# A bank pair emptied into a small tile, masks selected on POOL, and convolution steps that pause: a hybrid attention and mLSTM layer on one NeuronCore

## The chip, the core and the metric

The program runs on one core of a Trainium2 chip. The core has engines with queues of their own: PE (matmul, with its weight loads shown as PEld), DVE and ACT (elementwise work), POOL, and SP, which here only issues DMAs. PE writes its products to PSUM, eight banks of 512 fp32 columns; DVE and ACT read them there, POOL works on SBUF alone. The metric is the device time of one execution in microseconds.

## The reference

One encoder layer on two sequences of 1024 and 2048 tokens, each with the same 16 meta tokens ahead. After a norm, one projection feeds two branches, neighbourhood attention and a bidirectional mLSTM; their gated outputs are merged, projected and normed.

```python
xn = _rmsnorm(h, g_pre)
proj = xn @ w_in + b_in
na_q, na_k, na_v, na_z, ml_qk, ml_v, ml_z, ml_o, ml_g, mg = jnp.split(proj, SPLIT_IDX, axis=-1)
ya = (_neighbourhood_attention(na_q, na_k, na_v, na_rpb) * silu(na_z)) @ w_a
yb = (_mlstm_branch(ml_qk, ml_v, ml_g, ml_o, ml_conv_w, ml_head_g) * silu(ml_z)) @ w_b
y = (ga * ya + gb * yb) @ w_out
return h + _rmsnorm(y, g_post)
```

The mLSTM branch first runs a convolution of three taps along the tokens over `ml_qk` and a SiLU. Then, in each direction, every chunk of tokens has a masked decay matrix and a state carried from the chunks before:

```python
logD = jnp.where(lower, b[..., :, None] - b[..., None, :] + ig[..., None, :], NEG)
S = jnp.einsum('bhnjd,bhnsd->bhnjs', q, k) * jnp.exp(logD - m_t[..., None])
num = einsum(S, v) + e_inter * einsum(Cs, q)
h = num / maximum(abs(den), exp(-m_t))
```

## The kernel before

**Precision.** Every fp32 operand is split into a rounded part and a rest (`h` and `l`: `xh` and `xl`, `whi` and `wlo`, `sh` and `sl`), ACT rounding and DVE subtracting, and PE forms two or three products of the parts (`mm3`, L180 to L182).

**Two streams.** `run` interleaves two generators. `dense` is the projection and the final products, by `PLAN`: a first group of columns of sequence 0, then the stage "S" (`sstream`), which computes the other columns of sequence 0 with seven products in place of eight, then the groups of sequence 1, then `final`. `sparse` is, by `STEPS`, the mLSTM of sequence 0, its attention, and the same two for sequence 1. PE's order is the order in which the code is written out; the order on the other engines is made by the planner, except that `behind` pins an instruction after the one traced before it on its engine. Each engine works through its queue in order.

**Steps between matmuls.** After every piece of a column job the code calls `beside` (L542), which advances work for the other engines. `pstep` (called at L545 and L547) advances one convolution by one step: `cprep` loads a stretch of `mq` or `mk`, waits some turns, scales by ACT (L1584), adds two taps by DVE (L1587), takes a tanh (L1589), multiplies (L1591) and stores to `qk`. Two convolutions are under way at a time. `cpreps` queues those of sequence 0 during the first group and those of sequence 1 when their columns are done.

**Splitting x.** `build_half` loads four parts of x for 512 tokens, scales them (L519), and after the word "scaled" splits each into `xh` (ACT, L526) and `xl` (DVE, L527). `sbegin` does the same for stage S.

**Stage S.** `sorder` sets the order of the units: 1, 6, 5, 2, 7 and so on for the first set of columns. `ssum` forms sums of weight quarters on DVE (L854), which ACT (L272) and DVE (L273) then split.

**mLSTM.** `ml_gates` makes the gate factors; for each of four heads `ml_states` makes the chunks' state sums and `ml_outputs` the outputs, in blocks `b` of two chunks of 128 tokens, five turns to a block. `load` fetches `um` (128 partitions, 2 chunks x 2 directions x 128); `mask` adds 0 or -1e30 to it (L1780), `decay` takes the exponential (ACT, L1786), `weigh` multiplies by the scores and splits (`sh`, `sl`). `back(b, j)` for each chunk writes the state's part to a `tr` bank and, by ACT with a factor (L1849), to `num`; then four products (L1852, L1853) fill `pa`, a pair of PSUM banks of which there is only one pair (the pool `pl`); DVE adds both halves of it to `num` (L1855, L1856). `finish` divides, `ml_norm` norms. The pair `pa` is also used in `ml_states`.

Of the kernel before, what the change touches and what calls it, by code (L numbers as in the profile page):

```python
# [10 lines left out]
F32 = mybir.dt.float32  # L11
F32R = mybir.dt.float32r
I32 = mybir.dt.int32
AF = mybir.ActivationFunctionType
ALU = mybir.AluOpType
# [3 lines left out]
P = 128  # L19
# [9 lines left out]
BIG = 1e30  # L29
# [8 lines left out]
CB = 2  # L38
# [88 lines left out]
class K:  # L127
# [3 lines left out]
    def __init__(self, tc, ins, outs):  # L131
        self.tc, self.nc = tc, tc.nc
        self.xs = []
        self.i, self.o = ins, outs
        self.wreq, self.wraw, self.wrdy, self.wout = deque(), deque(), deque(), 0
        self.wseen, self.wkept, self.xkept = set(), {}, {}
        self.rwait = {}
        self.xput, self.turn, self.last, self.turns = deque(), 0, None, False
        self.need, self.gpost = False, None
        self.pq, self.pact = deque(), deque()  # L140
        self.have, self.rtag = {}, "tr"
        self.fmend = {C_MK + 3 * P: "a", C_NK + 3 * P: "k", C_NQ + 3 * P: "q", C_NZ + 3 * P: "z"}
        self.bg, self.XF, self.XS, self.sb, self.staged = deque(), {}, {}, {}, deque()
        self.hold, self.early = deque(), True
        self.rpre, self.xhold = {}, True


    def rsqrt8(self, pool, v, shape):
# [304 lines left out]
    def build_half(self, s, t0, res):  # L453

        nc, wp = self.nc, self.wp
        if (s, t0) in self.xkept:
            yield
            yield "scaled"
            x = []
            for name, part in zip(("xh", "xl"), self.xkept[s, t0]):  # L460
                x.append(wp.tile([P, KT, HALF], F32R, name=name, bufs=2))
                for k in range(0, KT, 4):
                    nc.sync.dma_start(x[-1][:, k:k + 4, :512].bitcast(F32), part[:, k:k + 4, :])
                yield
            res.append(tuple(x))
            return
        if (s, t0) in self.XF:
            xts = [self.xfload(self.XF[s, t0], e) for e in range(4)]
            yield
            yield "scaled"  # L470
            x = self.xparts()
            for e in range(4):
                h = x[0][:, 2 * e:2 * e + 2, :512]
                self.behind(nc.scalar.activation(h, xts[e], AF.Copy))
                self.behind(nc.vector.tensor_tensor(x[1][:, 2 * e:2 * e + 2, :512], xts[e], h.bitcast(F32), op=ALU.subtract))
                yield
            res.append(tuple(x))
            self.xkeep(s, t0, x)
            return
        if s == 0:  # L480
            xts = self.xnext or [self.xtload(s, t0, e, wp, 4) for e in range(4)]
            self.xnext = None
            while self.rwait:
                yield "wait"
            self.early = False
            yield "scaled"
            g = self.gpre
            if not self.done:
                p = self.psum("sm", [P, 512])
                nc.tensor.matmul(p[:, :KT], self.ident, g, start=True, stop=True)  # L490
                g = self.cp.tile([P, KT], F32, name="gx")
                nc.vector.tensor_copy(g, p[:, :KT])
            x, r = self.xparts(), []
            for e in range(4):
                self.xsplit(x, xts[e], e, 0, g)
                if not self.done:
                    self.wflush(2)
                yield
            res.append(tuple(x))
            if self.done:  # L500
                return
            yield from self.rsum(self.toks, r)
            nc.vector.tensor_copy(self.rc[:, 4:8], r[0])
            dg = self.rdiag(r[0], self.toks[0][0])

            def rows():
                self.rrows(dg, self.rr[:, 1], "sm")
                self.xp.close()
            self.rwait[s, t0] = rows
        else:  # L510
            xts = [self.xtload(s, t0, e, wp, 4) for e in range(4)]
            yield
            yield
            rr = wp.tile([P, 512], F32, name="rx", tag="thT", bufs=1)
            self.rrows(self.rpre.pop((s, t0)), rr, self.rtag)
            yield
            for k in range(KT):
                v = xts[k // 2][:, k % 2]
                self.behind(nc.vector.scalar_tensor_tensor(v, v, self.gpre[:, k:k + 1], rr, op0=ALU.mult, op1=ALU.mult))  # L519
                if k % 2:  # L520
                    yield
            yield "scaled"
            x = self.xparts(t0 % 1024 == 0)
            for e in range(4):
                h = x[0][:, 2 * e:2 * e + 2, :512]
                self.behind(nc.scalar.activation(h, xts[e], AF.Copy))  # L526
                self.behind(nc.vector.tensor_tensor(x[1][:, 2 * e:2 * e + 2, :512], xts[e], h.bitcast(F32), op=ALU.subtract))  # L527
                yield
            res.append(tuple(x))
            self.xkeep(s, t0, x)  # L530

# [10 lines left out]
    def beside(self):  # L542

        self.turn += 1
        self.pstep()  # L545
        if (1, 0) in self.have:
            self.pstep()  # L547
        if self.bg and self.turn % 2 == 0:
            if next(self.bg[0], "end") == "end":
# [503 lines left out]
    def sstream(self, visits, nxt):  # L1053

        nc = self.nc
# [7 lines left out]
        for n, u in self.sorder(visits):  # L1063
            s, t0, c, v = self.sdq[n]
# [14 lines left out]
                            self.sstage(*visits[v + 1][:2], w)  # L1079
            q = self.sq[n]  # L1080
            if u == 7 and not n:
                self.sbload(1)
            tm = c in TMAJ
            form = ("p (k c) -> p k c", dict(k=4)) if tm else ("p (a k c) -> p a k c", dict(a=2, k=4))
# [95 lines left out]
    def group(self, s, t0, meta, cols, reuse, nxt):  # L1180
# [4 lines left out]
        for j, (kind, c) in enumerate(jobs):  # L1185
# [21 lines left out]
            for hf in range(2):  # L1207
# [2 lines left out]
                    side = self.spread(self.build_half(*todo[1][:2], self.xs), 15)  # L1210
                elif last and nxt and nxt[0] == "S":
                    if hf == 0:
                        while self.bg:
                            if next(self.bg[0], "end") == "end":
                                self.bg.popleft()
# [398 lines left out]
    def ml(self, s):  # L1614
# [3 lines left out]
        with tc.tile_pool(name=f"mg{s}", bufs=1, side="right", reuse_waits="tile") as keep:  # L1618
            with tc.tile_pool(name=f"mt{s}", bufs=1, side="right", reuse_waits="tile") as mp:
                self.tri = keep.tile([P, 2, P], F32, name="tri")  # L1620
                nc.sync.dma_start(self.tri, self.i["tri"])
                self.trim = keep.tile([P, CB, 2, P], F32, name="trim")
                for j in range(CB):
                    nc.sync.dma_start(self.trim[:, j], self.i["trimask"])
                g = []
                yield from self.ml_gates(s, keep, mp, g)
            self.small(False)
# [115 lines left out]
    def ml_outputs(self, mp, s, h, g, NB, sts, norms):  # L1743
# [33 lines left out]

        def mask(b):
            if b < NB:
                self.behind(nc.vector.tensor_tensor(ums[b], ums[b], self.trim, op=ALU.add))  # L1780

        def decay(b):
            if b < NB:
# [54 lines left out]
        def back(b, j):  # L1838
# [10 lines left out]
                nc.scalar.activation(num[:, j, d], pi[:, 130 * d:130 * d + 130], AF.Copy, scale=g[d]["e"][:, cc, h:h + 1])  # L1849
            pa = self.pl.tile([P, 2, 512], F32, name="pa")  # L1850
            for d in range(2):
                nc.tensor.matmul(pa[:, d, 0:258], sh[:, j, d, :], v[:, j].rearrange("p a c -> p (a c)")[:, 0:258], start=True, stop=True, skip_group_check=True)  # L1852
                nc.tensor.matmul(pa[:, d, 0:130], sl[:, j, d, :], v[:, j, 0], start=False, stop=True, skip_group_check=True)  # L1853
            nj = num[:, j]
            nc.vector.tensor_tensor(nj, pa[:, :, 0:130], nj, op=ALU.add)  # L1855
            nc.vector.tensor_tensor(nj[:, :, 0:P], pa[:, :, 130:258], nj[:, :, 0:P], op=ALU.add)  # L1856

        def finish(b):
            num = nums.pop(b)
# [429 lines left out]
```

## Time and profile before

| | |
|---|---|
| three runs: lowest, median, highest | 2721.04, 2722.5, 2722.78 us |
| the profiled execution, its own time | 2714.73 us |
| its span, from the first to the last instruction | 2713.0 us |
| instructions in the span | 47274 |

The profile is of one execution. Its page gives busy times of each engine and the groups of instructions; the trace behind it gives each instruction's start, its duration, and, in brackets, how long its engine was idle just before it and which instruction ended that. A matmul's duration overlaps the next one's, so distances between starts are read where single gaps are meant. A line of the form `L1852` is a line of the kernel before.

### The profile page before, as it was taken

To read this page: it belongs to the slowest core of one execution; us is meant where nothing else is said; L and a number is where in the kernel's file an instruction comes from. 1 tells how busy PE (TensorE), PEld (TensorE's weight loads), DVE (VectorE), ACT (ScalarE), POOL (GpSimd) and SP (SyncE) were. 2 spreads that over 40 slices of the span, in tenths; PEclk is the share of its full clock that TensorE was granted. 3 is DMA by queue.
4 is the path that set the end of the run, shared out by engine and by line. 5 is a ranking of instruction groups with operands and counts; after the bars stand their busy time and mean duration, and the time that the engine had idled before them with its cause. 6 is when DMAs were issued, how large, how long until landed. Compare 5 with 4: busy or idle time off the path is not lost.

```text
span 2713.0 us, 47274 instructions
## 1 busy us (share of the span) xinstructions
PE 2671.5 (98%) x16504; PEld 2376.4 (88%) x16504; DVE 1792.7 (66%) x4424; ACT 1517.0 (56%) x3375; POOL 124.8 (5%) x294
## 2 busy tenths in 40 slices
PE   9999999999999999999999999999999999999998
PEld 7999988879998789998878888888889898989888
DVE  5557765545777746775424868575668879787764
ACT  5233354435555556666534756565548676777641
POOL 0005000005000004000000000000000000000000
PEclk9999999999999999999999999999999999999999
DMA  9984454369865797766576666786589999898955
GB/s 375 338 280 140 141 191 153 101 236 344 268 216 175 249 333 219 216 209 198 183 261 200 212 232 205 234 295 205 177 291 339 316 304 296 250 324 245 314 210 220
DMA packets 351507, 657.51 MB, mean 242 GB/s; under 512 B 53445, under 2 KB 158869, under 8 KB 351269
## 3 DMA queue, kind: packets, MB, share of 16 engines
q1 hardware_dynamic: 344004, 645.46, 71.4%
q0 software_dynamic: 7264, 9.04, 1.2%
q8 instruction: 130, 2.13, 0.3%
q14 instruction: 109, 0.88, 0.1%
HBM read 438.64 MB, written 215.66 MB: 241 GB/s over the span
## 4 chain that ended last, share of the span: by engine, by line
PE 82%; DMA 8%; DVE 6%; ACT 3%; issue 1%; SPq 0%; POOL 0%; DVEq 0%; ACTq 0%; POOLq 0%
PE pj L180 13%; PE pj L181 13%; PE pj L182 13%; PE pj L658 5%; PE pj L660 5%; PE pj L659 5%; PE sm L1424 2%; PE pj L2066 2%; PE pj L2064 2%; PE pj L2065 2%; PE tr L1410 2%; DMA tg<-gt 1%; PE pa L1852 1%; DMA kr<-nkm 1%; PE sm L182 1%
## 5 line engine op out<-in xcount | busy, mean ns | idle before, releaser
L180 PE MATMUL pj<-xh,whi 128*128 128x512 f32 (+1 forms) x1480 | 581.2, 393 | 3.8 <-ACT st L581 2.4
L181 PE MATMUL pj<-xl,whi 128*128 128x512 f32 (+1 forms) x1480 | 566.6, 383 | 0.4 <-DVE xl L357 0.4
L182 PE MATMUL pj<-xh,wlo 128*128 128x512 f32 (+1 forms) x1480 | 565.7, 382 | 0.3 <-DVE wlo L284 0.3
L658 PE MATMUL pj<-whi,xh 128*128 128x256 f32 (+1 forms) x1152 | 330.8, 287 | 0.0
L182 PEld LDWEIGHTS pj<-xh,wlo 128*128 128x128 f32 x1480 | 278.8, 188 | 58.3 <-DVE wlo L284 0.5
L180 PEld LDWEIGHTS pj<-xh,whi 128*128 128x128 f32 x1480 | 278.8, 188 | 53.4 <-ACT st L581 3.1
L659 PE MATMUL pj<-wlo,xh 128*128 128x256 f32 (+1 forms) x1152 | 324.8, 282 | 0.0
L660 PE MATMUL pj<-whi,xl 128*128 128x256 f32 (+1 forms) x1152 | 324.8, 282 | 0.0
L181 PEld LDWEIGHTS pj<-xl,whi 128*128 128x128 f32 x1480 | 279.3, 189 | 46.5 <-issue 0.7
L2064 PE MATMUL pj<-whi,mh 128*128 128x256 f32 x768 | 219.8, 286 | 0.0
L658 PEld LDWEIGHTS pj<-whi,xh 128*128 128x128 f32 x1152 | 217.2, 189 | 0.4
L659 PEld LDWEIGHTS pj<-wlo,xh 128*128 128x128 f32 x1152 | 217.1, 188 | 0.2
L660 PEld LDWEIGHTS pj<-whi,xl 128*128 128x128 f32 x1152 | 217.0, 188 | 0.0
L2065 PE MATMUL pj<-wlo,mh 128*128 128x256 f32 x768 | 216.5, 282 | 0.0
L2066 PE MATMUL pj<-whi,mlo 128*128 128x256 f32 x768 | 216.5, 282 | 0.0
L1413 DVE TENSOR_TENSOR pts<-tr,pts 96x384 fp32r<-96x384 f32 (+2 forms) x192 | 118.5, 617 | 65.4 <-ACT pts L1412 64.6
L180 PE MATMUL pj<-yh,whi 128*128 128x512 f32 x384 | 154.1, 401 | 0.7 <-ACT yh L1436 0.7
L181 PE MATMUL pj<-yl,whi 128*128 128x512 f32 x384 | 151.0, 393 | 0.2 <-DVE yl L1437 0.2
L182 PE MATMUL pj<-yh,wlo 128*128 128x512 f32 x384 | 151.0, 393 | 0.0
L2065 PEld LDWEIGHTS pj<-wlo,mh 128*128 128x128 f32 x768 | 145.5, 189 | 1.0
L2064 PEld LDWEIGHTS pj<-whi,mh 128*128 128x128 f32 x768 | 145.4, 189 | 1.0
L2066 PEld LDWEIGHTS pj<-whi,mlo 128*128 128x128 f32 x768 | 145.4, 189 | 0.0
(459 smaller groups left out, 6106.8 us busy)
## 6 DMA issues: line engine op xcount, KB each, us to landing
whi<-wh SPq DMA_DIRECT2D x140, 512.0 KB
wlo<-wl SPq DMA_DIRECT2D x140, 512.0 KB
wraw<-wu SPq DMA_DIRECT2D x64, 512.0 KB
wh<-whi SPq DMA_DIRECT2D x64, 512.0 KB
wl<-wlo SPq DMA_DIRECT2D x64, 512.0 KB
gt<-st SPq DMA_DIRECT2D x96, 256.0 KB
tg<-gt SPq DMA_DIRECT2D x96, 256.0 KB
xt<-xt SPq DMA_DIRECT2D x32, 512.0 KB
```

Source lines behind the costliest of these rows:

```text
L180: mm(out, ah, bh, start=start, stop=False, **more)
L181: mm(out, ah, bl, start=False, stop=False, **more)
L182: mm(out, al, bh, start=False, stop=stop, **more)
L658: nc.tensor.matmul(o, xh, wh, start=k == 0 and not (pair and a), stop=False, skip_group_check=True)
L659: nc.tensor.matmul(o, xh, wl, start=False, stop=False, skip_group_check=True)
L660: nc.tensor.matmul(o, xl, wh, start=False, stop=k == KT - 1, skip_group_check=True)
L1410: nc.tensor.transpose(pt[:ks, ch, :], pr_[:, ch * ks:(ch + 1) * ks], self.ident)
L1413: nc.vector.tensor_tensor(pts[:ks, :nb, 1, :], pt[:ks, :nb], pts[:ks, :nb, 0, :].bitcast(F32), op=ALU.subtract)
L1424: nc.tensor.matmul(av[:, cb % 2], vt[:ks, kc // 8 + ch].rearrange("p a b -> p (a b)"), pts[:ks, ch].rearrange("p a b -> p (a b)"), start=c ...
L2064: nc.tensor.matmul(o, mh[:, f, xs], q, start=fresh and f == 0, stop=False, skip_group_check=True)
L2065: nc.tensor.matmul(o, mh[:, f, xs], w[1][:, k, :], start=False, stop=False, skip_group_check=True)
L2066: nc.tensor.matmul(o, ml[:, f, xs], q, start=False, stop=f == KT - 1, skip_group_check=True)
```

## The change

- `back` makes the first of its products 260 wide in place of 258, copies the second half of `pa` with ACT into a new tile `hl` of 128 x 2 x 130 (one buffer), adds the first half of `pa` to it with DVE, and adds the sum to `num` with a DVE instruction that reads SBUF alone.
- `mask` no longer adds the constant `trim`: for each direction POOL selects between `um` and -1e30 by position. The loads of `trim` go.
- A flag `quiet` stops the calls of `pstep` in `beside`: in `build_half`, for tokens that are scaled there, while the four parts of x are split; and from the last column job ahead of stage S to unit 7 of its first set.
- In `beside`, `pstep` is called a third time per turn once the mLSTM of sequence 0 is done.

```diff
         self.turn += 1
-        self.pstep()
-        if (1, 0) in self.have:
+        for _ in range(0 if self.quiet else 1 + ((1, 0) in self.have) + (("ml", 0) in self.done)):
             self.pstep()
...
             yield "scaled"
             x = self.xparts(t0 % 1024 == 0)
+            self.quiet = True
             for e in range(4):
...
                 yield
+            self.quiet = False
             res.append(tuple(x))
...
             if u == 7 and not n:
+                self.quiet = False
                 self.sbload(1)
...
                     if hf == 0:
+                        self.quiet = True
                         while self.bg:
...
-                self.trim = keep.tile([P, CB, 2, P], F32, name="trim")
-                for j in range(CB):
-                    nc.sync.dma_start(self.trim[:, j], self.i["trimask"])
...
             if b < NB:
-                self.behind(nc.vector.tensor_tensor(ums[b], ums[b], self.trim, op=ALU.add))
+                for d in range(2):
+                    u = ums[b][:, :, d]
+                    nc.gpsimd.affine_select(u, u, [[0, CB], [1 - 2 * d, P]], ALU.is_ge, -BIG, base=0, channel_multiplier=2 * d - 1)
...
-                nc.tensor.matmul(pa[:, d, 0:258], sh[:, j, d, :], v[:, j].rearrange("p a c -> p (a c)")[:, 0:258], start=True, stop=True, skip_group_check=True)
+                nc.tensor.matmul(pa[:, d, 0:260], sh[:, j, d, :], v[:, j].rearrange("p a c -> p (a c)"), start=True, stop=True, skip_group_check=True)
                 nc.tensor.matmul(pa[:, d, 0:130], sl[:, j, d, :], v[:, j, 0], start=False, stop=True, skip_group_check=True)
             nj = num[:, j]
-            nc.vector.tensor_tensor(nj, pa[:, :, 0:130], nj, op=ALU.add)
-            nc.vector.tensor_tensor(nj[:, :, 0:P], pa[:, :, 130:258], nj[:, :, 0:P], op=ALU.add)
+            both = mp.tile([P, 2, 130], F32, name="hl", bufs=1)
+            nc.scalar.activation(both, pa[:, :, 130:260], AF.Copy)
+            nc.vector.tensor_tensor(both, pa[:, :, 0:130], both, op=ALU.add)
+            nc.vector.tensor_tensor(nj, both, nj, op=ALU.add)
```

## What I predicted

> **What bounds the kernel now.** I read the page's engine rows first, then the table of engines by stage, then the list of PE's waits, and last the timelines around the longest of them.
>
> ```profile
> span 2713.0 us, 47274 instructions
> PE 2671.5 (98%) x16504; PEld 2376.4 (88%) x16504; DVE 1792.7 (66%) x4424; ACT 1517.0 (56%) x3375; POOL 124.8 (5%) x294
> ```
> ```profile
> 195.00:215.00 20.00, 17.07 (x116) 15.15 (x115) 16.14 (x24) 11.22 (x18) 0.00 (x0) 1.00 0.68 220
> 215.00:612.00 397.00, 397.00 (x2203) 340.80 (x2202) 240.78 (x371) 169.66 (x260) 37.16 (x85) 1.00 0.49 161
> 912.00:930.00 18.00, 12.55 (x51) 10.21 (x50) 17.00 (x43) 12.74 (x28) 1.48 (x6) 0.81 0.49 155
> 930.00:1400.00 470.00, 470.00 (x3060) 428.17 (x3060) 274.72 (x656) 271.33 (x559) 39.58 (x93) 1.00 0.71 228
> 1490.00:1985.00 495.00, 486.62 (x2484) 406.76 (x2483) 344.54 (x1126) 305.97 (x800) 2.79 (x10) 1.00 0.67 219
> ```
>
> PE is busy for 2671.5 of 2713.0 us, so whatever leaves PE's own work alone can win at most the 41.5 us between. The columns of the stages are: stretch, its length, busy time of PE, PEld, DVE, ACT and POOL, granted clock, DMA share, GB/s. From 215 to 612 and from 930 to 1400 PE has no gap at all; nothing done to another engine there can help. The gaps that this change can reach lie in three places: the first seven-product units (195 to 215, 2.9 us idle), the split of x under the first sequence's mLSTM (912 to 930, 5.5 us idle and a mean clock of 0.81), and the mLSTM of the second sequence (1490 to 1985, 8.4 us idle).
>
> ```profile
> L1852 PE MATMUL pa<-vh,sh 128*128 128x258 f32 x192 | 51.3, 318 | 13.8 <-DVE num L1856 9.1 <-DVE mv L1927 2.8 <-DVE mv L1929 1.6
> PE pa L1852 <- DVE num L1856: 9.1, 8, 5.3
> ```
>
> One matmul, L1852, owns 13.8 us of the idle time: it writes the single bank pair `pa`, which must first be emptied. The longest wait is 5.3 us, so the others come to 8.5 us.
>
> **A, the first seven-product units.** The flag `quiet` is raised at the last column job of the first group and lowered at unit 7, so no convolution step is issued in between.
>
> ```profile
> 200.79 0.28 PE L1096 MATMUL pj<-whi,xh 128*128 128x256 f32 x1
> 201.70 0.39 PE L1097 MATMUL pj<-wlo,xh 128*128 128x256 f32 x1 [0.63 <-DVE wlo L273]
> ...
> 208.05 0.28 PE L1018 MATMUL tr<-whi,xmm 128*48 128x256 f32 x1
> 208.17 0.28 PE L1019 MATMUL tr<-wlo,xmm 128*16 128x256 f32 x1
> 209.65 0.35 PE L1096 MATMUL pj<-whi,xh 128*128 128x256 f32 x1 [1.20 <-DVE sn L976]
> 211.10 0.39 PE L1097 MATMUL pj<-wlo,xh 128*128 128x256 f32 x1 [1.10 <-DVE wlo L273]
> ```
> ```profile
> 205.26 0.53 ACT L1584 ACTIVATE cp<-cp,cw 128x272 f32<-128x272 f32 x1 [4.88 <-DMA cp<-mk]
> ```
> ```profile
> 205.82 0.51 DVE L1587 SCALAR_TENSOR_TENSOR cp<-cp,cw 128x272 f32<-128x272 f32 x1 [2.31 <-ACT cp L1584]
> 206.24 1.22 DVE L854 TENSOR_TENSOR t<-b,b 128x1024 f32<-128x1024 f32 x1
> ```
>
> Undisturbed, such matmuls start 0.12 us apart (208.05 to 208.17), so three gaps lose (0.91 + 1.48 + 1.45) - 3 x 0.12 = 3.5 us. Their cause stands in the last rows: DVE sat 2.31 us behind a convolution that waited for ACT, which waited for the convolution's own load; the weight sum `t` of L854 was queued behind it, and its split (L273) ends the third gap; the second lies right after `t`, too. With no convolution there `t` can start about 2.3 us earlier, and SP no longer has convolution loads ahead of the weight loads. The removed steps are not saved, only issued after unit 7, beside products that keep PE busy without a gap (215 to 612, no gap). I take 3.0 of 3.5 us.
>
> **B, the split of x at 912 to 930.** The same flag is raised while `build_half` splits the four parts of x.
>
> ```profile
> 918.60 0.28 PE L182 MATMUL tr<-cch,qkx 128*128 128x260 f32 x1
> 924.22 0.55 PE L1852 MATMUL pa<-vh,sh 128*128 128x258 f32 x1 [5.34 <-DVE num L1856]
> ```
> ```profile
> 920.25 0.62 ACT L1584 ACTIVATE cpl<-cpl,cw 128x400 f32<-128x400 f32 x1
> 920.77 1.13 ACT L1849 ACTIVATE num<-tr,g_eT 128x130 f32<-128x130 f32 x4
> ```
> ```profile
> 921.62 0.62 DVE L1587 SCALAR_TENSOR_TENSOR cpl<-cpl,cw 128x400 f32<-128x400 f32 x1
> 922.17 0.41 DVE L1855 TENSOR_TENSOR num<-pa,num 128x260 f32<-128x260 f32 x1
> ...
> 923.66 0.41 DVE L1856 TENSOR_TENSOR num<-pa,num 128x256 f32<-128x256 f32 x1
> ```
> ```profile
> 924.30:929.60 5.30, 5.30 (x15) 0.50 0.47 140
> 929.70:935.00 5.30, 5.30 (x29) 1.00 0.92 293
> ```
>
> The wait is 924.22 - 918.60 - 0.12 = 5.5 us. Behind it the clock is 0.50 until about 929.7, and 1.00 after that: of the 5.5 us from 924.2 on, half, 2.7 us, go too. Together 8.2 us hang on this one event. Bounds: if the two convolutions seen here were issued before the flag rises, only the new emptying acts: `num` done at about 921.3, the copy to 921.7, one addition behind L1587 at 922.2 to 922.7, that is 1.4 us earlier than 924.07 (923.66 + 0.41). If they are held, ACT comes to `num` half a microsecond sooner and no L1587 stands ahead of the addition: the copy is done at about 921.2, the addition at 921.6, 2.5 us earlier than 924.07, and the slow stretch need not come: 2.5 + 2.7 = 5.2 us. The most is all 8.2. I take 5.0, because with the flag raised the second of these cases is what the code asks for.
> The Trainium skill ("TensorE: Matmul & The Clock Gate", Part 1) says that the clock halves after one idle window of about 3.4 us. By that rule any wait cut below that length gets back all 2.7 us at once, and 1.4 us of shortening would be worth 4.1.
>
> **C, the bank pair.** Now ACT copies the second half of `pa` into a 260-wide tile, DVE adds the first half to it, and that addition frees the pair; the addition to `num` reads SBUF only. Before, both DVE additions (L1855, L1856) had to be done, the first only after ACT had written `num`.
>
> ```profile
> 1645.47 0.28 PE L1852 MATMUL pa<-vh,sh 128*128 128x258 f32 x1
> ...
> 1648.97 0.28 PE L182 MATMUL tr<-cch,qkw 128*128 128x260 f32 x1
> 1650.44 0.35 PE L1852 MATMUL pa<-vh,sh 128*128 128x258 f32 x1 [1.19 <-DVE mv L1927]
> ```
> ```profile
> 1647.64 0.42 DVE L1855 TENSOR_TENSOR num<-pa,num 128x260 f32<-128x260 f32 x1
> ...
> 1648.75 1.21 DVE L284 TENSOR_TENSOR wlo<-wraw,whi 128x1024 fp32r<-128x1024 f32 x1
> 1649.88 0.42 DVE L1856 TENSOR_TENSOR num<-pa,num 128x256 f32<-128x256 f32 x1
> ```
>
> Here 1649.88 - 1647.64 - 0.42 = 1.8 us of other DVE work slipped between the two additions, and PE waited 1650.44 - 1648.97 - 0.12 = 1.35 us. With one addition the pair is free at about 1648.1, before PE asks. Where ACT itself is late, as at 920, the extra copy takes back what the second addition gives: 0.38 us of ACT (next row but one) for 0.42 us of DVE. So between nothing and 8.5 us (below nothing is rival 1); I take half, 4.2, as the two events shown are one of each kind. The copy waits for the pair's last product, and behind it on ACT stand the rounding of the state and the column jobs' evacuations, each 0.4 us later at most. The small tile is single, so a copy also waits for the addition to `num` of the pair before, which was issued a good 3 us earlier.
>
> ```profile
> L1780 DVE TENSOR_TENSOR um<-um,trim 128x512 f32<-128x512 f32 x48 | 32.7, 682 | 2.8 <-DMA um<-ud 2.8
> L1823 ACT ACTIVATE ss<-sc 128x256 f32<-128x256 f32 x48 | 18.1, 378 | 50.4 <-PE sc L1821 50.4
> L1794 DVE TENSOR_TENSOR vh<-va,vh 128x260 fp32r<-128x260 f32 x48 | 20.2, 422 | 8.7 <-ACT vh L1793 8.6
> ```
>
> In work: ACT gains 96 copies x 0.38 = 36.5 us, DVE keeps two additions of 0.42 each (the one from SBUF by L1794) and loses 32.7 us of masks. The two products grow from 258 to 260 columns: 2/258 of 51.3 us, 0.4 us at the most.
>
> **D, the masks on POOL, and the third step.** 48 additions of 0.68 us become 96 selections of 128x256 on POOL. None is in the trace.
>
> ```profile
> L1195 POOL CAST xmm<-xh 128x128 fp32r<-128x128 f32 x2 | 0.6, 349 | 3.3 <-ACT xh L403 3.3
> L1726 POOL MEMSET st<- 128x130 f32 x8 | 1.7, 208 | 529.2 <-DVE ccl L1812 518.6 <-PE sm L181 10.6
> L598 POOL COPY km<-st 128x16 f32<-128x16 f32 x4 | 2.3, 579 | 16.7 <-ACT st L581 16.5
> L1051 POOL DMA_DIRECT2D nv<-stT x128 | 71.1, 563 | 154.0 <-DVE stT L678 83.6 <-DVE vwl L1692 55.1 <-DMA nv<-stT 5.7
> ```
>
> Bounds: 0.2 us each (the fill of 130) and 9.3 us (the copy of 16 columns scaled up, 0.579 x 16). The nearest row is the cast of 128 columns, twice it is 0.7 us; I take that. The exponentials need the mask two of a block's five turns later, about 3.6 us by the distance of a block's two `pa` products (1645.47 to 1648.97 + 0.12), and 2 x 0.7 fits in. The selection waits for `um`'s load, issued a block before. Behind a selection on POOL stand only the `nv` stores (0.56 us each, in 612 to 672) and fills. The four mask loads that go were 128 KB each on SP's queue, worth nothing. From `("ml", 0)` on a third convolution step is issued per turn: the same work sooner, in the stretch 930 to 1400 where PE has no gap and DVE is busy 58%. It costs nothing unless that cover fails. D and the wider products together: 0.2 us lost.
>
> **Sum.** 3.0 + 5.0 + 4.2 - 0.2 = 12.0 us off the profiled execution (2714.73 us, span 2713.0), so 2702.7 there. The median shown, 2722.5, lies 7.8 us above that execution; I subtract the same 12.0 and forecast 2710.5.
>
> **Rivals.**
> 1. ACT takes DVE's place. In 1490 to 1985 ACT is busy 62% and DVE 70%; moving 24 us to ACT (64 copies) and taking 22 off DVE (32 masks) turns them to 67% and 65%. For it: at 920 and in half the waits `num` on ACT is what is late. Against: the exponentials need no longer wait for DVE. C and B give nothing, A remains: 2719.5.
> 2. The selections are late (the slower side). Place: `um` before the exponentials of all 48 blocks, above all in 612 to 672 behind the `nv` stores, which wait for PE's own output. It decides from 1.8 us for one selection (2 x 1.8 = 3.6). At 2.15 us each block loses 0.7 us, 34 in all, less A and B: +26, so 2748. At the far bound of 9.3 us it would be hundreds. Against: twice the cast row is a third of that.
> 3. Selections and DVE get in each other's way, as both read SBUF: 96 x 0.7 = 67 us of DVE blocked against 32.7 removed; if one tenth of the 34 us reaches PE, C is gone and 3.4 lost: 2714.5 + 3.4 = 2717.9. No row of before has POOL reading beside DVE. The Trainium skill ("SBUF — State Buffer", Who interferes with whom) says that a DVE instruction with two SBUF inputs contends with a POOL instruction that reads SBUF, which is this case; no run here shows it yet.
> 4. The pause doesn't do what it says at B: the convolutions were issued before. B is 1.4: 2722.5 - 3.0 - 1.4 - 4.2 + 0.2 = 2714.1.
>
> **How the numbers follow.** Forecast 0.51, rival 1 0.17, rival 2 0.09, rival 3 0.08, rival 4 0.15. A measurement of this kernel tells about 0.2% (5.4 us) from no change. The forecast and rival 4 (-8.4 us) are faster: 0.66; rivals 1 and 3 lie within: 0.25; rival 2 is slower: 0.09. The range goes from all that the three places hold (3.5 + 8.2 + 8.5 = 20.2 us, and 3 more for waits that move by chance) to no change: 2699 to 2723. It leaves out rival 2 and a little of the others.
>
> **What would show it.** A: no gap over 0.3 us among L1096 and L1097 at the first units. B: no clock under 1.00 near 920, and a wait of L1852 there of 3 us or less. C: L1852's idle time falls from 13.8 to about 5 us. D: selections of about 0.7 us, and no idle time of ACT behind them at the exponentials. Wrong if L1852 now waits behind ACT's copies, if a new gap opens between 930 and 1230, or if the gap at 918 stands.

## The result: slower by 0.7%, and the profile after

| | before | after |
|---|---|---|
| median of the runs on one chip | 2722.64 us (4 runs, 2721.04 to 2726.46) | 2739.38 us (4 runs, 2738.30 to 2743.47) |
| ratio after to before, 95% interval | | 1.0068 [1.0054, 1.0083] |
| the profiled execution, its own time | 2714.73 us | 2743.47 us |
| its span | 2713.0 us | 2741.7 us |

I forecast 2710.5 us, in a range of 2699 to 2723, and gave "slower" 9 chances in 100. The medians lie 16.7 us apart the other way. The two profiled executions lie 28.7 us apart, because that of before happens to be 8 us under its median and that of after 4 us over its own; so stages are compared by their pattern, and totals by the medians.

The engine rows of the page of after: DVE lost 16 us of work, ACT gained 26, POOL has 96 instructions and 45 us more. No engine has become the bound; PE is still busy 98% of the span.

```profile
span 2741.7 us, 47530 instructions
...
PE 2679.5 (98%) x16504; PEld 2382.4 (87%) x16504; DVE 1776.3 (65%) x4376; ACT 1542.8 (56%) x3471; POOL 170.2 (6%) x390
```

The table of engines by stage of after (columns as before: stretch, length, busy time of PE, PEld, DVE, ACT, POOL, granted clock, DMA share, GB/s):

```profile
195.00:215.00 20.00, 20.00 (x145) 18.72 (x145) 13.93 (x16) 10.19 (x12) 0.00 (x0) 1.00 0.36 102
...
612.00:700.00 88.00, 78.33 (x634) 77.60 (x634) 51.62 (x154) 44.99 (x122) 38.84 (x73) 0.94 0.84 290
...
905.00:950.00 45.00, 42.37 (x206) 35.02 (x205) 35.96 (x89) 29.33 (x68) 3.30 (x10) 0.96 0.65 220
950.00:1100.00 150.00, 142.67 (x932) 130.42 (x931) 93.42 (x226) 85.61 (x179) 36.78 (x68) 0.99 0.85 267
```

The first row is step A as it was meant: no idle time of PE is left. The second and the fourth are new losses, in stretches where before had nearly none: 9.7 us idle between 612 and 700 with a clock of 0.94, and 7.3 us idle between 950 and 1100.

PE works through the same 16504 matmuls in the same order in every kernel here, so a stage can be measured from one matmul to another, whatever the clock time. This table is worked out from the starts of the same matmuls in each trace; it gives the change of a stage's length against before, in us. Stages are named by before's times; 1100 to 1400, where nothing moved, is left out. 0 to 195, which no edit touches, shows how much moves by chance.

| stage | after | after, two steps | after, masks on DVE | after, first head's masks on DVE | small tile alone | pause alone | early pause (last experiment) |
|---|---|---|---|---|---|---|---|
| 0 to 195 | +0.3 | +0.8 | +0.1 | +1.3 | +2.9 | +0.8 | +0.7 |
| 195 to 215 | -3.7 | -3.7 | -3.7 | -3.7 | +1.1 | -3.7 | -3.7 |
| 215 to 612 | +0.1 | 0.0 | 0.0 | 0.0 | 0.0 | +0.1 | 0.0 |
| 612 to 700 | **+12.0** | +12.6 | -0.6 | -0.6 | -0.6 | 0.0 | -0.6 |
| 700 to 905 | +2.2 | +3.1 | -0.7 | -1.1 | -1.6 | -0.4 | -1.6 |
| 905 to 950 | -3.9 | -3.6 | -1.5 | -0.7 | -2.2 | +0.7 | -3.7 |
| 950 to 1100 | **+10.0** | 0.0 | +3.5 | +1.2 | +1.9 | 0.0 | 0.0 |
| 1400 to 1985 | +3.6 | +1.9 | -4.5 | +3.4 | -4.6 | +0.6 | -3.8 |
| 1985 to the end | +8.4 | +6.4 | +2.6 | +3.9 | +1.2 | +1.8 | +4.6 |

Where the 12 us between 612 and 700 went is seen in three timelines of after around 680 (start, duration, engine, line, out<-in, count; in brackets the idle time ahead and what ended it). PE:

```profile
679.63 0.28 PE L182 MATMUL tr<-cch,qkx 128*128 128x260 f32 x1
...
689.44 0.58 PE L1854 MATMUL pa<-vh,sh 128*128 128x260 f32 x1 [9.53 <-ACT sh L1836]
```

POOL:

```profile
664.39 2.77 POOL L1052 DMA_DIRECT2D nv<-stT  x5 [0.95 <-DVE stT L679]
668.42 1.81 POOL L1052 DMA_DIRECT2D nv<-stT  x3 [1.27 <-DMA nv<-stT]
670.24 1.54 POOL L1782 TENSOR_SCALAR_AFFINE_SELECT um<-um 128x256 f32<-128x256 f32 x4
```

ACT:

```profile
680.46 0.63 ACT L1851 ACTIVATE num<-tr,g_eT 128x130 f32<-128x130 f32 x2 [0.48 <-DVE hb L1878]
684.89 1.65 ACT L1940 ACTIVATE hb<-hb,nb,nwy 128x128 f32<-128x128 f32 x4 [3.81 <-DVE nb L1938]
686.44 2.43 ACT L1788 ACTIVATE um<-um,g_a 128x128 f32<-128x128 f32 x8
688.78 0.61 ACT L1836 ACTIVATE sh<-um 128x512 fp32r<-128x512 f32 x1
```

PE waits 9.5 us for `sh`. The four selections of two blocks came behind eight `nv` stores on POOL and were done at 671.8 (670.24 + 1.54); yet their eight exponentials (L1788) ran at 686.4, because in ACT's queue they stood behind the norm (L1940), which waited 3.8 us for a chain of small DVE instructions. ACT itself was idle meanwhile. The half clock behind the wait is the rest of the 12 us: the granted clock is 0.50 until 695.1, which takes about half of the 5.7 us from 689.4 on.

### The profile page after: what moved, and what is told of

It reads as the page before. It is cut to its first block, busy times and chain, and to the rows that moved or that the text cites. A ratio compares the mean times of both kernels' runs of the same rounds, so it can differ in the third digit from the quotient of the medians.

```text
span 2741.7 us, 47530 instructions
## 1 busy us (share of the span) xinstructions
PE 2679.5 (98%) x16504; PEld 2382.4 (87%) x16504; DVE 1776.3 (65%) x4376; ACT 1542.8 (56%) x3471; POOL 170.2 (6%) x390
```

## The experiments

All ratios are to the kernel before on the same chip, with 95% intervals; medians of different rows can come from different chips, so rows are compared by their ratios. "After" in an edit means the changed kernel. The theory at the start, Q: the selections cost by where they, and the exponentials behind them, stand in the queues of POOL and ACT. The rivals: P, they cost by their length or by getting in DVE's way in SBUF; and T, it is the third convolution step that costs.

| kernel | median us (runs) | ratio |
|---|---|---|
| after | 2739.38 (4) | 1.0068 [1.0054, 1.0083] |
| after, two steps | 2732.93 (5) | 1.0046 [1.0031, 1.0060] |
| after, masks on DVE | 2711.47 (9) | 0.9961 [0.9948, 0.9975] |
| before + small tile | 2718.09 (10) | 0.9993 [0.9980, 1.0006] |
| before + pause | 2716.23 (10) | 0.9987 [0.9975, 1.0000] |
| before + third step | 2723.00 (10) | 1.0012 [0.9998, 1.0026] |
| after, exponentials in written order | 2734.69 (4) | 1.0061 [1.0044, 1.0077] |
| the same, and the norm | 2731.11 (5) | 1.0039 [1.0024, 1.0054] |
| after, exponentials written right behind the selections | 2736.57 (5) | 1.0048 [1.0032, 1.0064] |
| after, nv stores on SP | 2775.12 (4) | 1.0187 [1.0164, 1.0209] |
| both of the last two | 2767.94 (4) | 1.0163 [1.0143, 1.0183] |
| after, first head's masks on DVE | 2719.54 (10) | 0.9995 [0.9983, 1.0007] |
| the same, exponentials right behind the masks | 2721.10 (10) | 0.9995 [0.9985, 1.0005] |
| after, masks on DVE, two steps | 2709.04 (4) | 0.9963 [0.9948, 0.9978] |
| the same, early pause | 2706.80 (4) | 0.9959 [0.9944, 0.9974] |

**1. One part undone, or one part alone.** The third step undone:

```diff
-        for _ in range(0 if self.quiet else 1 + ((1, 0) in self.have) + (("ml", 0) in self.done)):
+        for _ in range(0 if self.quiet else 1 + ((1, 0) in self.have)):
```

> The changed kernel without its third convolution step per turn. Theory (the third step puts a convolution's first ACT instruction at the head of ACT's queue before its load has landed, and attention waits behind it): the waits of PE in the first sequence's attention (about 1019 to 1097 us after the start in the changed kernel: 1.3 + 4.0 + 2.2 + 0.7 = 8.2 us beyond the usual distance) go, and the time falls by 6 to 10 us against the changed kernel, to about +8 against before. Rival (those waits come from how the planner reshuffled everything): they stay within 3 us and the time falls by under 3 us.

The masks back on DVE, pinned as they were, with a constant of half the size (one chunk, repeated over both):

```diff
-                for d in range(2):
-                    u = ums[b][:, :, d]
-                    nc.gpsimd.affine_select(...)
+                self.behind(nc.vector.tensor_tensor(ums[b], ums[b], <trim, repeated over the chunks>, op=ALU.add))
```

> The changed kernel with the masks back on DVE (a constant of half the size, read twice, since the whole one and the small tile don't fit together). Theory (the masks stand behind the nv stores on POOL, so the exponentials of the first head were put behind the norm on ACT): the 9.7 us wait of PE at about 680 us and the half-clock stretch behind it, 12 us together, go, and the time falls by 8 to 12 us against the changed kernel. Rival A (the wait comes from the small tile's extra ACT work): it stays over 5 us. Rival B (POOL's selections block DVE wherever both read SBUF): DVE's mean times per instruction fall by several per cent in the mLSTM stages against the changed kernel.

The small tile alone on before (with the half-size constant), and the flag alone on before:

> The kernel before with the bank pair emptied into the small tile alone (masks stay on DVE, with the constant of half the size read twice). Prediction's step C: L1852's idle time falls from 13.8 to about 9 us, the time by about 4 us. Rival (ACT takes DVE's place): the idle time of the product into pa stays at 12 to 15 us, and the time is within 3 us of before.

> The kernel before with the pause alone. Prediction's steps A and B: the three gaps between 200 and 212 us go (3.5 us), and the wait at 918 us falls from 5.5 to about 3 us with no half-clock stretch: 8 us less in all. Rival 4 (the two convolutions there were issued ahead of the flag): only A comes, 3 to 4 us, and the convolutions still stand beside the split of x at 912 to 924 us.

The masks on POOL cost 1.0068 - 0.9961, about 1.1% or 28 us: without them the change is a gain. That is more than twice the 8 to 12 us expected, for besides the wait at 680 other stages came back too, 950 to 1100 and 1400 to 1985 above all. The third step costs 1.0068 - 1.0046 in after, 6 us, and the whole of the +10.0 us between 950 and 1100 goes with it in the profile. These two costs can't be added: the masks alone, with the third step left in, also take that stage from +10.0 to +3.5. The small tile and the pause alone can't be told from no change by their times, but their traces tell what each did. The list of groups of the small tile alone has the idle time of the first product into `pa` (the last column) at 4.2 us, where before had 13.8 and after, which has the same tile, has 16.6, of them the 9.5 of the one wait above; the first row below is the small tile alone, the second after:

```profile
L1851 PE MATMUL pa<-vh,sh 128*128 128x260 f32 x192 | 50.3, 313 | 4.2 <-DVE hl L1856 2.4 <-DVE nwy L154 1.2 <-DVE vh L1793 0.5
```
```profile
L1854 PE MATMUL pa<-vh,sh 128*128 128x260 f32 x192 | 51.3, 317 | 16.6 <-ACT sh L1836 9.5 <-DVE hl L1859 3.3 <-DVE vh L1796 2.2
```

The pause alone took the 3.7 us at the first seven-product units, but the wait of step B stands as before, 5.3 us in PE's list of waits, and DVE's timeline there still has convolutions (L1590) between the parts of x (L528):

```profile
PE pa L1855 <- DVE num L1859: 10.0, 9, 5.3
```
```profile
912.13 1.22 DVE L528 TENSOR_TENSOR xl<-xt,xh 128x1024 fp32r<-128x1024 f32 x1
...
913.93 0.63 DVE L1590 SCALAR_TENSOR_TENSOR cpl<-cpl,cw 128x400 f32<-128x400 f32 x1
...
915.55 1.22 DVE L528 TENSOR_TENSOR xl<-xt,xh 128x1024 fp32r<-128x1024 f32 x1
...
918.42 0.63 DVE L1590 SCALAR_TENSOR_TENSOR cpl<-cpl,cw 128x400 f32<-128x400 f32 x1
918.97 0.42 DVE L1858 TENSOR_TENSOR num<-pa,num 128x260 f32<-128x260 f32 x1
```

The third step alone on before:

> The kernel before with the third convolution step alone. If it costs by itself: gaps of 3 to 10 us in all between 950 and 1100, where PE had none, and ratio 1.001 to 1.004. If it hurt only together with the other edits: no gap there, ratio 0.999 to 1.001.

It opens a gap of 2.0 us at 1082 and lengthens 950 to 1100 by 3.5 us, but the ratio, 1.0012, is not clear of 1. How it costs is seen in the groups of ACT: the scaling of a convolution (L1587) stands idle on its own load. A convolution waits a fixed count of steps between load and scaling, so a third step per turn leaves its load a third less time, and ACT, which works in order, then stands with the attention's exponentials behind it. In after, without the third step, and the same pair with the masks on DVE:

```profile
L1587 ACT ACTIVATE cpl<-cpl,cw 128x384 f32<-128x384 f32 (+2 forms) x48 | 26.1, 573 | 36.6 <-DMA cpl<-mk 12.7 <-DMA cpl<-mq 12.2 <-DMA whi<-wh 6.8
```
```profile
L1587 ACT ACTIVATE cpl<-cpl,cw 128x384 f32<-128x384 f32 (+2 forms) x48 | 25.6, 572 | 21.3 <-DMA cpl<-mk 13.8 <-DMA xh<-xh 5.0 <-DMA cpl<-mq 2.4
```
```profile
L1587 ACT ACTIVATE cpl<-cpl,cw 128x384 f32<-128x384 f32 (+2 forms) x48 | 26.1, 573 | 24.4 <-DMA cpl<-mk 9.1 <-DMA cpl<-mq 8.9 <-DMA mk<-st 5.2
```
```profile
L1587 ACT ACTIVATE cpl<-cpl,cw 128x384 f32<-128x384 f32 (+2 forms) x48 | 25.5, 572 | 8.6 <-DMA cpl<-mq 4.5 <-DMA cpl<-mk 3.9
```

The third step adds some 15 us of that idle time each time. One such stand in after, SP's timeline first, then ACT's and PE's. The profile names another load (`vr`) as what ended ACT's wait; that ACT stood for the convolution's own load is inferred, since L1587 reads nothing that comes from `vr`, and SP had issued two convolution loads 3.9 us before:

```profile
1026.75 0.93 SPq L1582 DMA_DIRECT2D cpl<-mk  x2
```
```profile
1030.65 1.12 ACT L1587 ACTIVATE cpl<-cpl,cw 128x384 f32<-128x384 f32 x2 [4.43 <-DMA vr<-nvm]
...
1034.47 0.58 ACT L1396 ACTIVATE prb<-sm,mx 128x384 f32<-128x384 f32 x1 [0.80 <-DVE mx L1392]
```
```profile
1030.94 0.49 PE L1413 MATMUL tr<-ident,prb 128*96 128x128 f32 x3
1035.19 0.74 PE L1427 MATMUL sm<-pts,vt 96*128 96x256 f32 x4 [3.76 <-ACT prb L1396]
```

**2. The order on ACT alone.** If Q is right, putting the exponentials in their place should win most of the 28 us back. First they were kept in written order (`behind`), then the norm's instructions too:

```diff
-    nc.scalar.activation(ums[b][:, j, d], ums[b][:, j, d], AF.Exp, ...)
+    self.behind(nc.scalar.activation(ums[b][:, j, d], ums[b][:, j, d], AF.Exp, ...))
...
-    nc.scalar.activation(hb[:, j], hb[:, j], AF.Identity, ...)
+    self.behind(nc.scalar.activation(hb[:, j], hb[:, j], AF.Identity, ...))
```

> The kernel after, with the exponentials of um (ACT, L1788) kept on ACT in the order in which they are written; the selections stay on POOL. Theory Q (the masks cost by where the exponentials stand in ACT's queue: some 20 us ahead of their use, so that ACT stands behind a selection whose load is not there yet): ACT's idle time behind the selections falls from 66.9 to under 25 us, the stages from 1400 on get back their 4 to 10 us, and the time falls to 2722 to 2732; the loss of 12 us between 612 and 700 stays, since there another piece of work (the norm, L1940) stands ahead of the exponentials. Theory P (the selections themselves, their length or the ports that POOL and DVE share): nothing but the order of ACT is changed, so 2735 to 2743 as for the kernel after (2739.4).

> As the last, and the norm's four instructions on ACT (L1940) kept in written order too, which puts the exponentials of the third and fourth block ahead of them. Theory Q: the wait of 9.5 us of L1854 for sh at 680 falls under 3 us, the half clock after it goes, and with the gain of the last kernel the time comes to 2710 to 2718, within 5 us of the masks on DVE (2711.5), though all 96 selections stay on POOL. Theory P: 2735 to 2743.

Both expectations of Q failed by their times, 1.0061 and 1.0039, where Q asked for a gain of two thirds. But P fails for the second as well: with nothing changed except the order on ACT it gained 1.0068 - 1.0039, some 8 us, 3.8 of them between 612 and 700 (+8.2 against +12.0). The pins worked, but written order is no good order: around 680, in the timelines of the second kernel (POOL, ACT, PE), the selections were done at 676.1, the exponentials still stood behind other work of ACT until 683.7, and PE still waited 6.4 us:

```profile
674.40 1.68 POOL L1782 TENSOR_SCALAR_AFFINE_SELECT um<-um 128x256 f32<-128x256 f32 x4
```
```profile
683.17 0.63 ACT L1851 ACTIVATE num<-tr,g_eT 128x130 f32<-128x130 f32 x2 [0.48 <-DVE hb L1878]
683.69 2.44 ACT L1788 ACTIVATE um<-um,g_a 128x128 f32<-128x128 f32 x8
```
```profile
688.92 0.58 PE L1854 MATMUL pa<-vh,sh 128*128 128x260 f32 x1 [6.37 <-ACT sh L1836]
```

Then the exponentials were written two turns earlier, right behind the selections, and kept there:

```diff
             mask(b + 1)
+            decay(b + 1)
             chain(b)
...
-            decay(b + 1)
```

> The kernel after, with the exponentials of um written right behind the selections of their block (two turns earlier than the last attempt, which put them 1 to 3 us ahead of their use) and kept there on ACT; selections and nv stores stay on POOL. Theory Q (place in ACT's queue): between 700 and 1985 the stages come within 3 us in all of the kernel with the masks on DVE, the 12 us between 612 and 700 stay, and the time is 2724 to 2731. Theory P (length of the selections, ports): as the two pinned kernels or worse, 2731 to 2740.

The stages from 1400 to 1985 came from +3.6 us in after to -1.6, two thirds of the way to the -4.5 of the masks on DVE, but the total hardly followed: 1.0048, with a median of 2736.57 where Q asked for 2724 to 2731, and 612 to 700 still at +11.7, where the planner went on putting the exponentials of two blocks behind the norm.

**3. The stores ahead of the selections.** The `nv` stores were moved to SP, alone and with the last edit:

```diff
-                    self.nc.gpsimd.dma_start(dst, st[...])
+                    self.nc.sync.dma_start(dst, st[...])
```

> The kernel after, with the stores of nv (L1052) issued by SP in place of POOL, so that nothing but selections and fills is on POOL between 612 and 700. If the 12 us lost there come from the selections standing behind these stores (on POOL itself, and in the planner's reckoning, which then puts the exponentials of two blocks behind the norm): the wait of 9.5 us of L1854 for sh goes under 2 us, the half clock after it too, and the time is 2725 to 2731; what is lost in the other stages stays. If the selections are slow or late by themselves: the wait stays over 6 us, and the time 2735 to 2743.

> Both of the last two edits. Theory Q: with the order on ACT and on POOL mended the 96 selections cost next to nothing, and the time is within 5 us of the kernel with the masks on DVE (2711.5): 2709 to 2717. Theory P: the selections and what they do to DVE are all still there, so 2725 or more.

Much slower, for a new reason: SP's queue takes 8.65 us for the eight stores at 682 (first row), and the loads of other work stand behind them, among them the bias `bb` (second row), which DVE needs for `stT`. PE (third row) then waits 15 us for `stT`, and 19 us a second time:

```profile
682.34 8.65 SPq L1052 DMA_DIRECT2D nv<-stT  x8
693.00 0.42 SPq L636 DMA_DIRECT2D bb<-b_in  x1
```
```profile
699.38 0.59 PE L659 MATMUL pj<-whi,xh 128*128 128x264 f32 x1 [15.14 <-DVE stT L676]
```

By their times these two runs don't tell Q from P. But the trace of the first answers a part of the question. Nothing but the stores' queue was changed, all selections are on POOL, and yet the exponentials of all four blocks of the first head are back in their place: they start before the last selection of their block has ended, and ahead of the norm (the third block here, POOL's timeline first, then ACT's). PE's longest wait for `sh` there is 1.1 us, in place of 9.5.

```profile
677.47 0.94 POOL L1782 TENSOR_SCALAR_AFFINE_SELECT um<-um 128x256 f32<-128x256 f32 x2 [9.91 <-DMA nv<-stT]
```
```profile
678.09 1.28 ACT L1788 ACTIVATE um<-um,g_a 128x128 f32<-128x128 f32 x4 [1.54 <-POOL um L1782]
...
700.69 1.65 ACT L1940 ACTIVATE hb<-hb,nb,nwy 128x128 f32<-128x128 f32 x4
```

**4. Four blocks of 48.** So the place was taken away in another way: the first head of sequence 0, the only one that runs beside the `nv` stores, gets its masks from DVE; the other 44 blocks keep their selections.

```diff
+                if (s, h) == (0, 0):
+                    self.behind(nc.vector.tensor_tensor(ums[b], ums[b], <trim, repeated>, op=ALU.add))
+                    return
                 for d in range(2):
```

> The kernel after, with the masks of the first head of sequence 0 (4 of 48 blocks, those that run beside the nv stores on POOL) added by DVE as before; the other 44 blocks stay with POOL's selections, the nv stores stay on POOL. If the loss between 612 and 700 is one of place (selections behind the nv stores, exponentials then put behind the norm): the wait of L1854 for sh at 680 goes, that stage comes from +12.0 to within 1 us of before, and the time falls by 8 to 14 us from the kernel after, to 2725 to 2731. If each selection costs by its length or by the ports: a twelfth of the cost goes, 1 to 3 us, so 2736 to 2739.

The ratio is 0.9995 against 1.0068: some 20 of the 28 us hang on these four blocks, more than Q had asked for. In the table 12.6 us of the gain lie between 612 and 700 and 8.8 between 950 and 1100, where the third step is still in and 44 selections are still on POOL; why that second stage came back is not shown. The first has no idle time and no half clock left:

```profile
612.00:700.00 88.00, 88.00 (x737) 87.73 (x736) 58.11 (x178) 51.08 (x137) 35.77 (x65) 1.00 0.93 319
```

Last, the order of the other 44 blocks' exponentials was mended as in `decay` right behind `mask`:

> The same, and the exponentials of all blocks written right behind their masks and kept there on ACT, with 88 selections still on POOL. Theory Q (place in the queues): 612 to 700 within 1 us of before, 700 to 1985 (without the third step's 950 to 1100) near the -5 us of the masks on DVE, and the time 2715 to 2723, so that at least two thirds of the 28 us are back while eleven twelfths of the selections are still there. Theory P (length, ports): 2731 or more.

Its time lies in Q's range, but the last kernel's did already: the new order won nothing in all, 0.9995 again. The groups of ACT show that it did what it should: the idle time ahead of the exponentials fell from 73.4 us (first row, without) to 9.8 us (second row, with). The stages from 1400 to 1985 were 4 us shorter for it (-0.7 against +3.4), 905 to 950 were 3.8 us shorter, and other stages as much longer. So taking away 64 us of ACT's idle time behind the selections shows in single stages, but not in the total, which the intervals hold to some 4 us.

```profile
L1793 ACT ACTIVATE um<-um,g_a 128x128 f32<-128x128 f32 x192 | 63.0, 392 | 73.4 <-POOL um L1787 64.2 <-DVE um L1783 8.9
```
```profile
L1793 ACT ACTIVATE um<-um,g_a 128x128 f32<-128x128 f32 x192 | 63.6, 393 | 9.8 <-DVE um L1783 9.0 <-POOL um L1787 0.8
```

**5. What is left of the change, and a better pause.** Masks on DVE and two steps; and the same with the flag raised some turns earlier, before x is scaled, so that the two convolutions that get in at step B are issued after the split:

```diff
+            self.quiet = True
             for k in range(KT):
                 v = xts[k // 2][:, k % 2]
```

> The kernel after with the masks on DVE (constant of half the size) and without the third convolution step. If the third step costs by itself, as it did between the kernel after and the one without it (6.5 us), the 3.5 us lost between 950 and 1100 go and the time is 2705 to 2709. If it cost only together with the selections, 2711.5 as for the masks on DVE, give or take 2.

> As the last, and the flag is raised before x is scaled (about 4 turns earlier), so that the first two convolutions of sequence 1 are issued after the split. If the pause failed at the split of x because these two convolutions were issued before it: no convolution on ACT or DVE between the x parts, the waits of 1.9 and 1.1 us at 919 and 921 shrink to under 1 us together, the clock stays 1.00, and the time is 2 to 5 us below the last kernel. If the parts of x alone hold up ACT and DVE there: within 1 us of the last kernel.

0.9963 and 0.9959: both are faster than before and after, and the two can't be told apart. Without the third step the 3.5 us between 950 and 1100 went in the profile, but the time, 0.9963 against 0.9961, doesn't show it. In the trace the early pause kept the convolutions out from between the parts of x, and 905 to 950 is 2.0 us shorter (-3.7 against -1.7 us), but a wait of 2.8 us is left there, not under 1 us, and the clock behind it is not 1.00.

## Why the prediction was wrong, step by step

**A held.** Taken 3.0 us; the stage became 3.7 us shorter in every kernel with the pause, and its 20.00 us have no idle time.

**B came, in part, and not by its reason.** The step that failed: "if they are held ... I take 5.0, because with the flag raised the second of these cases is what the code asks for". It was rival 4. The loads, the scaling and the taps of two convolutions are issued in the turns just ahead of the split, while the flag is down, and the engines reach them between the parts of x; with the pause alone the stage is +0.7 us and the wait of 5.3 us stands. What shortened it in after (-3.9 us) is in part C's tile, which alone gave -2.2 there; the other 1.7 us no run takes apart. Rival 4 put B at 1.4 us.

**C held in the place it named.** The idle time of the product into `pa` was to fall from 13.8 to about 5 us; with the tile alone it is 4.2, and 1400 to 1985, which holds the stage where the prediction found most of these waits, is 4.6 us shorter. Its time alone, 0.9993 [0.9980, 1.0006], holds the 4.2 us taken (0.9985), but holds zero as well.
A, B and C together, as in masks on DVE with two steps, measure 0.9963 [0.9948, 0.9978], 10 us less (6 to 14); the sum without D was 12.2.

**D was the miss: 0.2 us lost was taken, about 28 us were found for the masks.** The duration was no part of the error. The group of POOL has 0.48 us for one selection, below the 0.7 taken and far from the 1.8 us from which rival 2 was to decide:

```profile
L1782 POOL TENSOR_SCALAR_AFFINE_SELECT um<-um 128x256 f32<-128x256 f32 x96 | 44.1, 483 | 774.0 <-DMA um<-ud 260.1 <-DMA va<-mv 163.9 <-DMA wl<-wlo 78.2
```

What failed is this step: "The exponentials need the mask two of a block's five turns later ... and 2 x 0.7 fits in. Behind a selection on POOL stand only the `nv` stores". I asked what stands behind a selection, not what stands ahead of it; and I took the exponentials to stay where they were. Before, the mask was pinned on DVE by `behind`, and in the trace of before the exponentials followed it at once, about 12 us ahead of their use; the third block, DVE's timeline first, then ACT's:

```profile
660.77 0.68 DVE L1780 TENSOR_TENSOR um<-um,trim 128x512 f32<-128x512 f32 x1
```
```profile
661.49 1.28 ACT L1786 ACTIVATE um<-um,g_a 128x128 f32<-128x128 f32 x4 [1.36 <-DVE um L1780]
...
674.97 0.62 ACT L1834 ACTIVATE sh<-um 128x512 fp32r<-128x512 f32 x1
```

The selection has no pin and stands on another engine, so the planner set the exponentials anew: for two blocks beside the `nv` stores behind the norm, 14.7 us after their selections were done (671.8 to 686.4), and elsewhere about 20 us ahead of their use. The first cost most of it. Rival 2 had the place (612 to 672, behind the `nv` stores) and the sign, and its time, 2748, lies 9 us above the median; its mechanism, the length of a selection, did not occur.
Four of 48 blocks carry 20 of the 28 us; that is shown. That the stores on POOL's queue put their exponentials late is shown by the kernel with the stores on SP, where the same selections have theirs in place; by how much that order alone counts is not, since that kernel lost more elsewhere. What the other 44 selections cost, 0.9995 against 0.9961, about 9 us, stays open. In the profiles 7.9 us of it lie between 1400 and 1985, where these selections run (+3.4 against -4.5). Mending ACT's idle time behind them brought 4.1 us back there, but nothing in all, and the stages from 1985 on, where no selection runs, are 1.2 to 8.4 us longer in every kernel of the table, so a part may be order and chance.

**The third step**, taken at nothing, costs 6 us where all selections are on POOL (1.0068 against 1.0046, intervals that overlap a little), and nothing that the time shows where none is (0.9961 against 0.9963; alone 1.0012). The traces are clearer: in each of the three pairs the kernel with it is 3.5 to 10 us longer between 950 and 1100, and its twin without it is not. How much it costs hangs on the order around it: with the first head's masks on DVE it is still in, and the stage is only 1.2 us longer. The step that failed is "PE has no gap" between 930 and 1400, so that it "costs nothing unless that cover fails": the cover failed. That row says that nothing was late, not by how much; the convolutions' loads had their slack there, and the third step used it up.

**Rival 1** did not occur: with the 96 copies on ACT and the masks left on DVE the time is 0.9961.

**Rival 3, the ports.** The mechanism is there and its size isn't. In after's DVE timeline, while the four selections of 670.24 to 671.78 ran, two instructions with all inputs in SBUF took 1.78 us together, where the same pair at 679.72 took 0.64. The next row is an addition that reads PSUM and SBUF; this one began just after the last selection, but the nine of its kind that did overlap a selection took the usual 0.42 to 0.43 us as well:

```profile
670.14 1.78 DVE L1878 SCALAR_TENSOR_TENSOR hb<-num,den,hb 128x128 f32<-128x128 f32 x2 [0.53 <-ACT hb L1877]
671.85 0.42 DVE L1859 TENSOR_TENSOR hl<-pa,hl 128x260 f32<-128x260 f32 x1
```

Over all DVE instructions that overlap a selection, against the median of the same line elsewhere, this comes to some 6 us of DVE's 1776, where I had feared 34. The Trainium skill ("SBUF — State Buffer", Who interferes with whom) says that a DVE instruction with two SBUF inputs contends with a POOL instruction that reads SBUF; the trace agrees.

## What to carry to other kernels

When an instruction goes to another engine, its duration there is the smaller question: ask what stands ahead of it in the new queue at the moment it is needed, and what else the old place had held in order. Where a planner sets the order, read the place of the dependants in the new trace before reading any busy time; four blocks of 48 made the change a loss. An engine's idle time is no slack count: a stretch without gaps says nothing of how near its loads are to being late, and taking away 64 us of waiting on an engine off the path can leave the total as it was.

## What the runs showed of the hardware that I had not expected

The clock fell after waits shorter than the one at 918. In after, two waits of 1.9 and 1.1 us at 934 and 937 were followed by a clock of 0.71 (first row); with the early pause one wait of 2.8 us at 919 by 0.60 (second row); with the masks on DVE one of 2.7 us at 1074 by nothing at all (third row). These lengths are by the distances between starts; the idle times in brackets are 0.2 us less.

```profile
936.25 0.39 PE L180 MATMUL tr<-cch,qkx 128*128 128x260 f32 x1 [1.72 <-ACT num L1851]
937.79 0.56 PE L1854 MATMUL pa<-vh,sh 128*128 128x260 f32 x1 [0.91 <-DVE hl L1859]
```
```profile
921.81 0.36 PE L1855 MATMUL pa<-vh,sh 128*128 128x260 f32 x1 [2.63 <-DVE hl L1860]
```
```profile
1076.93 0.59 PE L1427 MATMUL sm<-pts,vt 96*128 96x256 f32 x3 [2.46 <-DVE yg L1434]
```

The clock behind them:

```profile
937.80:943.00 5.20, 5.20 (x20) 4.43 (x21) 3.10 (x9) 1.95 (x5) 0.20 (x2) 0.71 0.97 314
```
```profile
921.80:925.00 3.20, 3.19 (x11) 2.62 (x12) 2.64 (x10) 1.69 (x5) 0.00 (x0) 0.60 0.10 38
```
```profile
1077.00:1080.00 3.00, 3.00 (x25) 3.00 (x26) 2.84 (x7) 3.00 (x9) 0.00 (x0) 1.00 0.89 256
```

So the rule that I had cited, from the Trainium skill ("TensorE: Matmul & The Clock Gate", Part 1), a half clock after one idle window of about 3.4 us, does not carry to "any wait cut below that length gets its slow stretch back": here 2.8 us did not.

A store of `nv` takes SP no less time to issue than POOL: over the 128 stores the median is 0.57 us on SP and 0.56 on POOL, and the slowest on SP took 1.02 us. What cost was the place: everything else on SP's queue stood behind them.
